# A hybrid transformer block: pooling's products, pair outputs, the first gate operands and the left operands rearranged

## The chip, the cores and the metric

The kernel runs on one core of a Trainium2 chip. A time is the device time of one execution in microseconds (us). The kernel before took 1178.16 us, the median of three runs (1177.86 to 1179.1). About 0.2% is what a measurement of this kernel can tell from no change.

## The reference

One layer of a streaming encoder on 1024 tokens of width 1024, all in float32:

1. An RMSNorm, then one input projection whose columns feed three token mixers: causal pooling (four groups of 64 channels: trailing mean over 2, 4, 8 or 16 tokens minus the input, a 64 x 64 product per group, a scale), gated linear attention (4 heads of 64, chunks of 64, a gate and a norm per head) and forgetting attention (8 heads of 64, softmax of q k + F_t - F_s under a causal mask).
2. The mixers' outputs, 256 + 256 + 512 channels, go through the output projection w_o and are added to x.
3. A second RMSNorm, then a SwiGLU feed-forward of width 2816: silu(h Wg) * (h Wu) times W_down, added to x.
4. A last RMSNorm.

## The kernel before, in words

**Precision by splitting.** TensorE takes operands in a shorter float format here (fp32r). An operand is therefore split: the high part is a copy into that format (ScalarE), the low part the difference (VectorE or POOL, the subtract). A product is three matmuls: high x high, high x low, low x high (gemm, woven, L133 to L149). Each split costs ScalarE one pass and VectorE or POOL another.

**Buffers.** SBUF is cut into 33 general buffers of 128 x 1024 and some rings (L24 to L28). `G(name)` takes the first buffer of a first-in-first-out list, `free` puts it at the end, `R` goes round a ring. This happens when the program is written down, so which name follows which in a buffer is fixed there:

```
i = idle.pop(0)
t_ = big.tile([P, 1024], dtype, tag=f"g{i}", name=name)
```

A name waits for the name before it in its buffer to be finished with, transfers included.

**Order of the work.** A planner puts the instructions of each engine in order ahead of time, by a model of their durations: among those that it thinks ready, the one that stands first in the program goes first. On the chip each engine keeps that order. So matmuls of a later step fill holes of an earlier one where the planner saw them, and the program's order is a priority. All transfers but a few are issued by SyncE's queue (SP), in one order too: one that waits for its source or its buffer holds all behind it.

**PSUM** has eight banks: three "s", two "pt", one "o", two "gm". All input and output projections use the two "gm" banks.

**Stages** (names as in the profile):

- First norm and transposes (hT, in 16 buffers), the small projections gv and a (psg), decays.
- `pool_in` projects pooling's two halves (zp0, zp1). `pool_tile` (L476) builds the shifted sums on VectorE (ps2 to ps16), then d (pd), two matmuls with w_pool (py, L500), a scaled copy on ScalarE (L501), and `keep_mix` (L265), which splits the result and stores high and low parts in memory (mixs).
- Gated linear attention in two halves, A and B (class `Gla`): `keys` (zgk), `queries` (zgq), `gates` (zgg), and small work (turn_keys, state, within, outputs, turned) handed to the projections as `smalls`, which `woven` places between their matmuls.
- `fox_values(0)` (psv), with B's last outputs between; then `keep_wo` (L273) loads, splits and stores the eight blocks of w_o (wos0 to wos7, nine general buffers in turn).
- Forgetting attention, pairs 0 to 3 of heads: `fox_qk` (zq, zk: q's and k's high and low parts into six buffers q, k, kl), `fox_attend` with eight items a pair (s scores, pt transposes, o products). For pairs 0 to 2 each item's result (oy) is stored alone (L610, mixd); the split comes later in `load_mix` (L628: mr, mix). Pair 3 is split at once into last_mix.
- Output projection in two passes: `pxa` (mix 0 to 3) between the items of pair 3, `pxb` (mix 4 to 7), followed for each of eight blocks of tokens tb by the store x3d, `norm2` (sum of squares on ScalarE, the root by `rstd_D` on VectorE and POOL, n2sq on VectorE, transposes n2pt, copies hr).
- Gate and up projections by Strassen's seven products, 22 tiles fi: `right(fi)` loads two weight blocks and makes seven right operands (five sums, seven splits), `left(i)` makes the seven left operands hA from hr, `gate_up` multiplies (m, L767). Products 3 and 5 need only the first four blocks of tokens. `start(0)` stands at tb = 4, `start(1)` behind tb = 7.
- Down projection, again by seven products (d, L1007), and the last norm.

Of the kernel before, what the change touches and what calls it, by code (L numbers as in the profile page):

```python
# [9 lines left out]
F32 = mybir.dt.float32  # L10
# [21 lines left out]
def tile_hybrid_block(ctx: ExitStack, tc, x, w_fv, w_gv, w_zt, w_o, w_gu, w_down, ln, w_pool, w_a3, chans, b_f, consts, out):  # L32
# [51 lines left out]
    POOL.memset(mhalf, -0.5)  # L84
    ACT.preload_act_table_set("natural_log_exp_and_others")
# [10 lines left out]
    def rstd_D(ms, parts, name):  # L96

        v, r = S(f"{name}_v"), S(f"{name}_r")
        extra = ms[:, 1:2] if parts == 2 else 0.0
# [161 lines left out]
    mixd = dpool.tile([3, P, T], F32, name="mixd")  # L261
    mixs = dpool.tile([4, P, 2, T], F32, name="mixs")
    wod = dpool.tile([8, P, 2, D], F32, name="wod")

    def keep_mix(k, y):  # L265

        hi, lo = R(f"mh{k}", F32R), R(f"ml{k}", F32R)
        ACT.activation(hi, y, AF.Copy)
# [207 lines left out]
    def pool_tile(j, u):  # L476
# [15 lines left out]
        d = R(f"pd{j}")  # L492
# [3 lines left out]
        y = R(f"py{j}")  # L496
        for c in range(2):
# [3 lines left out]
            ACT.activation(y[:, csl], ps, AF.Copy, scale=ch[:, 4 + j:5 + j])  # L501
        keep_mix(j, y)
        free(f"u{j}")
# [34 lines left out]
    def fox_item(p, a, m, ops, fb, V):  # L538
# [68 lines left out]
        ACT.activation(ot, o[64:128, 0:256], AF.Copy)  # L607
        DVE.tensor_tensor(out=oy[rows], in0=o[0:64, 0:256], in1=ot, op=ALU.add)
        if p < 3:
            SP.dma_start(mixd[p, rows, m * 256:(m + 1) * 256], oy[rows])  # L610
        else:
# [4 lines left out]
    def fox_attend(p, ops, V):  # L616
# [5 lines left out]
        for a, m in ([(a, m) for a in range(2) for m in range(4)] if p < 3 else [(a, m) for m in (1, 0, 3, 2) for a in range(2)]):  # L622
            fox_item(p, a, m, ops, fbs[a], V)
# [4 lines left out]
    def load_mix(k0, g):  # L628

        mixes = []  # L630
        for k in range(k0, k0 + 4):
            if k == 7:
                mixes.append(last_mix[g])
                free(f"mr6_{g}")
                break
            t_ = G(f"mix{k}_{g}", F32R).rearrange("p (h t) -> p h t", h=2)
            if k < 4:
                SP.dma_start(f(t_), mixs[k, :, :, g * 512:(g + 1) * 512])
            else:
                if k % 2 == 0:  # L640
                    raw = G(f"mr{k}_{g}").rearrange("p (k t) -> p k t", k=2)
                src = raw[:, k % 2]
                SP.dma_start(src, mixd[k - 4, :, g * 512:(g + 1) * 512])
                ACT.activation(t_[:, 0], src, AF.Copy)
                POOL.tensor_tensor(out=t_[:, 1], in0=src, in1=f(t_[:, 0]), op=ALU.subtract)
                if k % 2:
                    free(f"mr{k - 1}_{g}")
# [28 lines left out]
    for k in range(8):  # L676
        keep_wo(k)
# [422 lines left out]
```

## Time and profile before

| | |
|---|---|
| median of three runs | 1178.16 us |
| the profiled execution, its own time | 1177.12 us |
| its span | 1175.4 us |
| mean granted TensorE clock | 0.99 |

A line of the timeline reads: start in us from the span's start, length, engine, line of the kernel, operation, result <- sources, shape, count, and in brackets the idle time of the engine before it with what ended it. A line of the list of waits reads: engine and line that waited <- what released it: total, number of times, longest. A line of grouped instructions reads: line, engine, operation, operands, count | busy us, mean ns | idle us before. "PEclk" or the column after the engines in a table of stages is the clock that TensorE was granted, 1.00 being full.

### The profile page before, as it was taken

The numbers are of one execution on the slowest core, as the hardware profiler recorded it, in microseconds if no ns is written. First come the engines' busy times: TensorE is split into PE (matmuls) and PEld (weight loads), VectorE is DVE, ScalarE is ACT, GpSimd is POOL, SyncE is SP. The second block draws the span as 40 slices with busy tenths as digits, with TensorE's granted clock in tenths as the row PEclk, the third lists the DMA queues.
The fourth block names the chain that finished last, engine by engine and source line by source line (L and its number), as shares of the span: only waits on it lengthen the run. The fifth ranks groups of instructions, "written<-read, shape, count | busy, mean of one in ns | idle before, by whom it ended". The sixth has DMA issues, their size and how long they took to land.

```text
span 1175.4 us, 16005 instructions
## 1 busy us (share of the span) xinstructions
PE 1136.0 (97%) x5928; PEld 958.5 (82%) x5928; DVE 827.2 (70%) x1342; ACT 531.3 (45%) x961; POOL 353.7 (30%) x267
## 2 busy tenths in 40 slices
PE   6989999999999999898999999999999999999996
PEld 6866888889988888786888888888888888888885
DVE  7596464288757766478998768777786685876686
ACT  6345234366655444455454434443343344334344
POOL 2112032342343323231112221022201271750693
PEclk9998999999999999998999999999999999999998
DMA  7122267211205733220333232332324688333233
GB/s 250 36 73 108 91 221 263 72 46 43 64 27 170 276 122 126 99 108 25 111 107 134 91 125 71 118 123 92 118 70 152 216 321 292 104 98 107 80 118 143
DMA packets 57981, 147.31 MB, mean 125 GB/s; under 512 B 5368, under 2 KB 7336, under 8 KB 57904
## 3 DMA queue, kind: packets, MB, share of 16 engines
q1 hardware_dynamic: 57472, 144.73, 36.0%
q0 software_dynamic: 432, 1.57, 0.4%
q8 instruction: 46, 0.75, 0.3%
q14 instruction: 31, 0.25, 0.1%
HBM read 103.52 MB, written 42.76 MB: 124 GB/s over the span
## 4 chain that ended last, share of the span: by engine, by line
PE 75%; DVE 3%; issue 1%; POOL 1%; DMA 1%; ACT 1%; POOLq 0%; ACTq 0%; DVEq 0%; SPq 0%
PE m L767 35%; PE d L1007 15%; PE pxa L138 3%; PE o L604 3%; PE pxb L138 3%; PE psv L146 2%; PE pt L590 2%; PE s L564 1%; PE s L565 1%; PE zq3p L146 1%; PE zk1p L146 1%; PE zq2p L146 1%; PE zk3p L146 1%; PE zq1p L146 1%; PE zk0p L146 1%
## 5 line engine op out<-in xcount | busy, mean ns | idle before, releaser
L767 PE MATMUL m<-hA_1h,wr 128*128 128x512 f32 x616 | 215.1, 390 | 0.0
L767 PE MATMUL m<-hA_0h,wr 128*128 128x512 f32 x616 | 214.9, 391 | 0.0
L767 PEld LDWEIGHTS m<-hA_0h,wr 128*128 128x128 f32 x616 | 116.1, 189 | 24.5 <-ACT hr L727 0.3
L767 PEld LDWEIGHTS m<-hA_1h,wr 128*128 128x128 f32 x616 | 116.0, 188 | 24.3
L751 ACT ACTIVATE wr<-ws 128x512 fp32r<-128x512 f32 x110 | 69.2, 632 | 119.6 <-DVE ws L750 59.3
L767 PE MATMUL m<-hA_0l,wr 128*128 128x512 f32 x308 | 120.3, 391 | 0.0
L767 PE MATMUL m<-hA_1l,wr 128*128 128x512 f32 x308 | 120.1, 390 | 0.0
L1007 PE MATMUL d<-lw,ha 128*128 128x512 f32 x308 | 119.8, 389 | 0.0
L1007 PE MATMUL d<-hw,ha 128*128 128x512 f32 x308 | 119.3, 389 | 0.0
L1007 PE MATMUL d<-hw,la 128*128 128x512 f32 x308 | 118.3, 389 | 0.0
L819 POOL TENSOR_TENSOR cg<-cu,cu 128x512 f32<-128x512 f32 x11 | 19.6, 1778 | 306.8 <-DVE cu L796 306.8
L752 DVE TENSOR_TENSOR wr<-ws,wr 128x512 fp32r<-128x512 f32 x110 | 78.2, 718 | 25.7 <-ACT wr L751 25.7
L873 DVE TENSOR_TENSOR la<-ra,ha 128x1024 fp32r<-128x1024 f32 (+1 forms) x42 | 57.3, 1370 | 27.9 <-ACT ha L872 20.8
L865 POOL TENSOR_TENSOR rw<-wd,wd 128x512 f32<-128x512 f32 x33 | 58.5, 1800 | 49.7 <-PE d L1007 49.6
L872 ACT ACTIVATE ha<-ra 128x1024 fp32r<-128x1024 f32 (+1 forms) x42 | 41.3, 987 | 65.8 <-DMA ra<-cd 62.3
L767 PEld LDWEIGHTS m<-hA_0l,wr 128*128 128x128 f32 x308 | 58.1, 189 | 12.0
L767 PEld LDWEIGHTS m<-hA_1l,wr 128*128 128x128 f32 x308 | 57.9, 188 | 12.0
L1007 PEld LDWEIGHTS d<-lw,ha 128*128 128x128 f32 x308 | 57.8, 188 | 12.1
L1007 PEld LDWEIGHTS d<-hw,ha 128*128 128x128 f32 x308 | 57.8, 188 | 12.0
L1007 PEld LDWEIGHTS d<-hw,la 128*128 128x128 f32 x308 | 57.8, 188 | 11.9
L579 POOL TENSOR_TENSOR pb<-pb,rl 128x128 f32<-128x128 f32 (+3 forms) x32 | 38.5, 1206 | 91.3 <-DVE rl L576 73.2
L573 ACT ACTIVATE pb<-pb,mn 128x128 f32<-128x128 f32 (+3 forms) x64 | 49.5, 774 | 34.1 <-DVE mn L569 33.9
(395 smaller groups left out, 2694.7 us busy)
## 6 DMA issues: line engine op xcount, KB each, us to landing
ra<-cd SPq DMA_DIRECT2D x35, 512.0 KB, 3.9
wg<-in_w_gu_dram SPq DMA_DIRECT2D x22, 512.0 KB, 3.6
wu<-in_w_gu_dram SPq DMA_DIRECT2D x22, 512.0 KB, 4.1
wd<-in_w_down_dram SPq DMA_DIRECT2D x22, 512.0 KB, 6.9
cd<-cg SPq DMA_DIRECT2D x11, 512.0 KB, 4.5
cd<-cs SPq DMA_DIRECT2D x11, 512.0 KB, 3.3
cd<-cu SPq DMA_DIRECT2D x11, 512.0 KB, 3.3
fb<-Fd SPq DMA_DIRECT2D x8, 512.0 KB, 3.8
```

Source lines behind the costliest of these rows:

```text
L138: PE.matmul(ps, a, b, start=(n == 0), stop=(n == last))
L146: PE.matmul(ps, a, b, start=(i == 0 and n == 0), stop=(i == len(terms) - 1 and n == 2))
L573: ACT.activation(pb[:, 0:W], pb[:, 0:W], AF.Exp, bias=mn[:, 0:1], scale=-1.0, accum_out=l[:, i:i + 1])
L579: POOL.tensor_tensor(out=pb[:, 0:W], in0=pb[:, 0:W], in1=rl[:, 0:1].broadcast_to([P, W]), op=ALU.mult)
L604: PE.matmul(*args, start=(kb == 0 and n_ == 0), stop=(last and n_ == 1))
L751: ACT.activation(hi, src, AF.Copy)
L752: e2.tensor_tensor(out=lo, in0=src, in1=f(hi), op=ALU.subtract)
L767: PE.matmul(ps, a, b, start=(n == 0), stop=(n == 11))
L865: POOL.tensor_tensor(out=raw_[:, j * 512:j * 512 + 512], in0=wd[h0, j0 + j][:, e0, :], in1=wd[h1, j0 + j][:, e1, :], op=op)
L872: ACT.activation(hi[:, sl], src, AF.Copy)
L873: DVE.tensor_tensor(out=lo[:, sl], in0=src, in1=f(hi[:, sl]), op=ALU.subtract)
L1007: PE.matmul(banks[t], a[:, o], b[:, ns], start=(j0 + j == 0 and m == 0), stop=(j0 + j == NF // 2 - 1 and m == 2))
```

## The change

- Pooling: `pool_tile` still makes d at its place, but the products, their copy and `keep_mix` are returned as two small works per half. Half 1's are handed to `A.gates`, half 0's to `B.queries`. pd, py and the high part mh become general buffers instead of ring buffers; `keep_mix` writes the low part over its input. `misc` is freed later.
- Pairs 0 to 2: each item adds its result into one general buffer y{p}; when the pair is through and the next pair's q and k stand in the program, `keep_mix(4 + p)` splits and stores it. `load_mix` then loads high and low parts, with no split.
- Right operands of gate tiles 0 and 1 are made behind `keep_wo` and ahead of `fox_qk(0)` and stored in a new array rwd; at the old place `fetch_right` loads them. Their sums move from POOL to VectorE.
- Left operands 1, 4, 2, 7 and 6 are made in two halves of the tokens.
- `norm2`'s root takes its addition on POOL.

```
+    def rstd_D(ms, parts, name, eng=None):
         v, r = S(f"{name}_v"), S(f"{name}_r")
+        if eng is POOL:
+            POOL.tensor_tensor(out=v, in0=ms[:, 0:1], in1=epst, op=ALU.add)
+            POOL.tensor_tensor(out=r, in0=v, in1=mhalf[:, 0:1], op=ALU.pow)
+            return r
...
     def keep_mix(k, y):
-        hi, lo = R(f"mh{k}", F32R), R(f"ml{k}", F32R)
+        hi = G(f"mh{k}", F32R)
         ACT.activation(hi, y, AF.Copy)
-        DVE.tensor_tensor(out=lo, in0=y, in1=f(hi), op=ALU.subtract)
+        DVE.tensor_tensor(out=y, in0=y, in1=f(hi), op=ALU.subtract)
         SP.dma_start(mixs[k, :, 0], f(hi))
-        SP.dma_start(mixs[k, :, 1], f(lo))
+        SP.dma_start(mixs[k, :, 1], y)
+        free(f"mh{k}")
...
+        free(f"u{j}")
+        y = []
+        def part(c):
+            if not y:
+                y.append(G(f"py{j}"))
             csl = slice(c * 512, c * 512 + 512)
             ps = PS("s", f"py{j}_{c}")
             PE.matmul(ps, wpb[:, j, :], d[:, csl], start=True, stop=True)
+            ACT.activation(y[0][:, csl], ps, AF.Copy, scale=ch[:, 4 + j:5 + j])
+            if c:
+                keep_mix(j, y[0])
+                free(f"pd{j}", f"py{j}")
+        return [lambda c=c: part(c) for c in range(2)]
...
+        if p < 3:
+            oy = Y[:, m * 256:(m + 1) * 256]
         DVE.tensor_tensor(out=oy[rows], in0=o[0:64, 0:256], in1=ot, op=ALU.add)
-            SP.dma_start(mixd[p, rows, m * 256:(m + 1) * 256], oy[rows])
...
+    RORDER = (3, 5, 4, 1, 2, 7, 6)
+    rwd = dpool.tile([2, 7, P, 1024], F32, name="rwd")
+    def right(fi, keep=False):
...
+                DVE.tensor_tensor(out=src, in0=in0, in1=in1, op=op)
+            ACT.activation(hi, src, AF.Copy)
+            DVE.tensor_tensor(out=lo, in0=src, in1=f(hi), op=ALU.subtract)
+            ops[i] = (hi, lo)
+            if keep:
+                SP.dma_start(rwd[fi, n], f(w_))
+                free(f"wr{fi}_{i}")
+    def fetch_right(fi):
+        ops = {}
+        for n, i in enumerate(RORDER):
+            w_ = G(f"wr{fi}_{i}", F32R)
+            SP.dma_start(f(w_), rwd[fi, n])
+            ops[i] = (w_[:, 0:512], w_[:, 512:1024])
+        return ops
...
             t_ = G(f"mix{k}_{g}", F32R).rearrange("p (h t) -> p h t", h=2)
-            if k < 4:
-                SP.dma_start(f(t_), mixs[k, :, :, g * 512:(g + 1) * 512])
-            else:
...
-                SP.dma_start(src, mixd[k - 4, :, g * 512:(g + 1) * 512])
-                ACT.activation(t_[:, 0], src, AF.Copy)
-                POOL.tensor_tensor(out=t_[:, 1], in0=src, in1=f(t_[:, 0]), op=ALU.subtract)
...
+            SP.dma_start(f(t_), mixs[k, :, :, g * 512:(g + 1) * 512])
...
-    pool_tile(1, us[1])
-    pool_tile(0, us[0])
-    free("misc")
+    pools = pool_tile(1, us[1]), pool_tile(0, us[0])
-    A.gates((A.state(), A.within(0)))
+    A.gates((A.state(), pools[0] + A.within(0)))
-    B.queries((A.turned(1), B.turn_keys()))
+    B.queries((A.turned(1) + pools[1], B.turn_keys()))
+    free("misc")
...
     for k in range(8):
         keep_wo(k)
+    for fi in range(2):
+        right(fi, keep=True)
     ops = fox_qk(0)
...
+        Y = G(f"y{p}") if p < 3 else None
+        fox_attend(p, ops, V, Y)
...
         if p < 3:
             free(*done)
+            keep_mix(4 + p, Y)
+            free(f"y{p}")
...
-        r = rstd_D(ss, 1, f"n2{tb}")
+        r = rstd_D(ss, 1, f"n2{tb}", POOL)
...
+            for c in (slice(0, 256), slice(256, 512)) if max(in0, in1 or 0) > 1 else (slice(0, 512),):
+                src = raw[in0][kp][:, :, c]
+                if in1 is not None:
+                    DVE.tensor_tensor(out=t_[:, :, c], in0=src, in1=raw[in1][kp][:, :, c], op=op)
+                    src = t_[:, :, c]
+                ACT.activation(hi[:, :, c], src, AF.Copy)
+                DVE.tensor_tensor(out=lo[:, :, c], in0=src, in1=f(hi[:, :, c]), op=ALU.subtract)
...
-        w_ = right(fi)
+        w_ = fetch_right(fi) if fi < 2 else right(fi)
```

More of the change, by code (lines that the diff above doesn't have):

```diff
@@ L84, in tile_hybrid_block @@
     POOL.memset(mhalf, -0.5)
+    epst = cst.tile([P, 1], F32, name="epst")
+    POOL.memset(epst, EPS)
     ACT.preload_act_table_set("natural_log_exp_and_others")
@@ L500, in pool_tile @@
             PE.matmul(ps, wpb[:, j, :], d[:, csl], start=True, stop=True)
-            ACT.activation(y[:, csl], ps, AF.Copy, scale=ch[:, 4 + j:5 + j])
-        keep_mix(j, y)
-        free(f"u{j}")
+            ACT.activation(y[0][:, csl], ps, AF.Copy, scale=ch[:, 4 + j:5 + j])
[3 more added lines that the diff above has]
+        return [lambda c=c: part(c) for c in range(2)]
     def fox_values(q, smalls=((),) * NT):
```

67 lines of the change are left out of this document (22 added, 45 removed).

## The prediction

> **What bounds the kernel now.** I read the page's first part, then the list of who waited for whom on TensorE, then the busy time in 20 us stages, and last the timeline around each hole.
>
> ```profile
> span 1175.4 us, 16005 instructions
> PE 1136.0 (97%) x5928; PEld 958.5 (82%) x5928; DVE 827.2 (70%) x1342; ACT 531.3 (45%) x961; POOL 353.7 (30%) x267
> ...
> PE n2pt L725 <- DVE n2sq L720: 4.6, 1, 4.6
> PE py L500 <- DVE pd L495: 4.4, 1, 4.4
> PE pxb L138 <- ACT mix L644: 2.8, 1, 2.8
> PE zgq0p L146 <- ACT gk L344: 2.4, 1, 2.4
> PE pxb L138 <- DVE xa L658: 1.5, 1, 1.5
> ```
>
> TensorE is busy for all but 39 us, so an edit pays only where it fills a hole of TensorE, and every new hole is paid in full. The five long waits that the edit could touch lie in three places: pooling (py and the zgq0p behind it), the start of the output projection's second half (pxb), and the end of the second norm (n2pt). The stages price them (columns: stage, its length, then busy time and instructions of PE, PEld, DVE, ACT and POOL, granted clock, DMA share, GB/s):
>
> ```profile
> 60.00:80.00 20.00, 20.00 (x89) 16.29 (x88) 19.53 (x15) 10.18 (x14) 5.82 (x3) 1.00 0.27 88
> 80.00:100.00 20.00, 13.25 (x40) 8.64 (x39) 15.51 (x23) 7.73 (x10) 1.90 (x1) 0.83 0.27 98
> ...
> 460.00:480.00 20.00, 14.62 (x96) 11.90 (x95) 11.07 (x16) 9.80 (x21) 7.19 (x9) 1.00 0.48 172
> 480.00:500.00 20.00, 20.00 (x90) 16.31 (x90) 8.80 (x13) 7.38 (x18) 6.36 (x7) 0.92 0.38 132
> ...
> 520.00:540.00 20.00, 15.41 (x78) 12.91 (x77) 15.57 (x18) 9.53 (x21) 9.24 (x8) 0.95 0.29 106
> 540.00:560.00 20.00, 20.00 (x81) 16.17 (x81) 18.38 (x19) 12.28 (x19) 0.00 (x0) 0.88 0.09 27
> 560.00:580.00 20.00, 20.00 (x90) 16.57 (x89) 18.64 (x26) 9.56 (x13) 1.68 (x1) 1.00 0.17 52
> ```
>
> An undisturbed stage starts 89 or 90 wide matmuls, so one costs 20/90 = 0.222 us. **Pooling's hole**: 40 instead of 89 starts, 20 x 49/89 = 11.0 us; about 1.0 of it is the pooling products' own work (the four passes take 1.88 us in a warm row below, against 4 x 0.222), so 10.0 us are lost, the low clock of 0.83 included. **The projection's hole**: 20 - 14.62 = 5.4 us idle, and 8% of the next 20 us at the clock of 0.92, 1.6 us: 7.0 us. **The norm's hole**: 20 - 15.41 = 4.6 us idle, 5% of that stage for its clock, 1.0, and 9 matmuls missing in the next, 2.0 us: 7.6 us. Together 24.6 us, the most that the edit can win at these places.
>
> **The change, part by part.**
>
> Pooling's products placed later:
>
> ```profile
> 87.44 3.62 PE L500 MATMUL py<-pd,misc 128*128 128x512 f32 x4 [4.40 <-DVE pd L495]
> 88.62 1.22 DVE L113 TENSOR_TENSOR zgg0l<-zgg0r,zgg0h 128x1024 fp32r<-128x1024 f32 x1
> 96.59 0.17 DVE L495 TENSOR_TENSOR pd<-ps,u 128x16 f32<-128x16 f32 x1
> 96.84 1.90 POOL L333 TENSOR_TENSOR d<-bc 128x1024 f32<-128x1024 f32 x1 [16.97 <-DMA mixs<-ml]
> 100.86 1.88 PE L500 MATMUL py<-pd,misc 128*128 128x512 f32 x4
> 108.99 1.90 POOL L333 TENSOR_TENSOR d<-bc 128x1024 f32<-128x1024 f32 x1 [10.25 <-DMA mixs<-ml]
> ```
>
> The first py waits for VectorE's chain of shifted sums, and behind it on TensorE stand the gated attention's queries; on ScalarE the copies of py stand ahead of the copy that empties gk's bank. The edit hands the products as small work into A.gates and B.queries, at least one projection later, so both waits go. No instruction is saved; the chain of sums stays where it is. What is late next is VectorE: the two chains end at 96.59 with the zgg0 split (1.22) between, while the queries now can start where the hole began, at 87.44 - 4.40 = 83.0, and end 48 x 0.222 = 10.7 us on, at 93.7. If the second chain goes first, the key product and that split come after it, and TensorE waits up to 3.5 us: 6.5 us won. If they slip between the sums, as the split at 88.62 did, all 10.0 are won. I take 9.0, nearer to that row. The halves d2 of the keys, POOL's L333, no longer stand behind stores of pooling's outputs in their ring of buffers, which helps.
>
> Pairs' outputs split per pair: the first three head pairs now collect their output in one buffer, are split once (ScalarE and VectorE, 1024 columns) and stored in two 512 KB transfers; before, 24 stores of 64 KB, and then at the reload a split by ScalarE and POOL.
>
> ```profile
> L644 ACT ACTIVATE mix<-mr x6: 630/633/635, 373.0 to 479.0; 128x512 fp32r<-128x512 f32 x6
> L645 POOL TENSOR_TENSOR mix<-mr,mix x6: 1277/1298/1306, 373.8 to 479.8; 128x512 fp32r<-128x512 f32 x6
> ...
> 455.68 0.80 SPq L643 DMA_DIRECT2D mr<-mixd  x2
> 461.33 0.37 SPq L283 DMA_DIRECT2D wo7h<-wod  x1
> ...
> SPq L643 <- PE o L604: 14.5, 1, 14.5
> ```
>
> The load of pair 2's half (mr) waited 14.5 us for TensorE's last attention product, since its buffer was the last pair's value buffer (names handed from a first-in-first-out list; I followed that list through the code). In the changed order the first half's three mix buffers are those of k3 and kl3, read by scores and not by the last products, and 0.63 + 1.30 us of splitting goes. The weights wo7 are still issued at 461.33, so products 6 and 7 cannot start before about 465; the attention's own latency remains. Of 7.0 I take 5.5, between 2.8 (the one wait named L644) and 7.0. VectorE gets three splits of 1.22 us more, off TensorE's path in pairs 0 to 2: nothing, or 3.7 us if each is waited for.
>
> The end of the norm: right operands gone from it, lefts in halves, POOL's add in the root:
>
> ```profile
> 529.63 2.31 DVE L720 SCALAR_TENSOR_TENSOR n2sq<-xa,n_r,ln2b 128x1024 f32<-128x1024 f32 x1 [0.44 <-POOL n_r L101]
> 530.32 0.39 PE L138 MATMUL pxb<-wo7h,mix 128*128 128x512 f32 x1
> 534.75 0.68 DVE L658 TENSOR_TENSOR xa<-pxb,xa 128x512 f32<-128x512 f32 x1
> 538.89 1.94 PE L725 MATMUL n2pt<-ident,n2sq 128*128 128x128 f32 x8 [4.59 <-DVE n2sq L720]
> ```
>
> The last projection ended at 530.7, but VectorE, filled with splits of right operands that wait for POOL, added it only at 534.75; from there to the transposes 4.14 us. Without those splits the add can come at 530.8 and the transposes at 530.8 + 4.14 + about 0.5 for POOL's extra add = 535.5. TensorE has four products of 12 matmuls that need only the first half of the tokens (48 x 0.222 = 10.7 us) as cover. I take 6.0 of 7.6, from 2.0 (VectorE's left operands late, a rival below) to 7.6. The 14 reloads of 512 KB go into a stage with a DMA share of 0.29 to 0.38.
>
> Making the right operands early is where the price lies. For two tiles: 4 loads, 10 sums and 14 low parts on VectorE (24 x 0.718 = 17.2 us), 14 copies on ScalarE, 14 stores, all between the stored w_o splits and the first q/k projection. That time is free on VectorE. The **buffers** are not. At this point nine of the list's buffers are in rotation: w_o's splits leave them, the right operands take them, and q0, k0 and kl0 are then given six that right operand 1 has just used. That names wait in the order of the program, even when a buffer is free, is shown by the two L333 rows above: POOL sat idle 16.97 and 10.25 us on tiles whose inputs were long there. So the copy of q0 out of its bank waits until tile 1's operands are made and stored:
>
> ```profile
> 200.54 0.32 SPq L276 DMA_DIRECT2D wod<-wos5h  x1
> 210.47 0.59 ACT L527 ACTIVATE q<-zq0p 64x512 fp32r<-64x512 f32 x1 [6.29 <-PE zq0p L146]
> 212.44 0.69 DVE L528 SCALAR_TENSOR_TENSOR q<-zq0p,q 64x512 fp32r<-64x512 f32 x1 [0.66 <-ACT q L527]
> 215.20 0.62 PE L146 MATMUL zk0p<-hT,zk0h 128*128 128x512 f32 x2
> ...
> L751 ACT ACTIVATE wr<-ws 128x512 fp32r<-128x512 f32 x110 | 69.2, 632 | 119.6 <-DVE ws L750 59.3
> L752 DVE TENSOR_TENSOR wr<-ws,wr 128x512 fp32r<-128x512 f32 x110 | 78.2, 718 | 25.7 <-ACT wr L751 25.7
> ...
> mixs<-ml SPq DMA_DIRECT2D x4, 512.0 KB, 3.1
> wu<-in_w_gu_dram SPq DMA_DIRECT2D x22, 512.0 KB, 4.1
> ...
> DMA to landing us min/median/max: 2.6/4.2/8.8
> ```
>
> The chain: wos5h's store is issued at 200.54 and lands 3.1 later; wu0 takes its buffer, 4.1; operand 3 takes 0.72 + 0.63 + 0.72 = 2.07 and operand 5 0.72 more, to 210.5; its store 3.1; wu1 takes that buffer, 4.1; operands 3 and 5 of tile 1, 2.8, to 220.5; store 3.1, to 223.6. q0's first half could go at 222.9 and its copies take 212.44 + 0.69 - 210.47 = 2.66: the bank is empty at 225.6. Both banks of this kind hold q0, so TensorE, which went on with zk0p at 215.20, now waits 10.4 us. Behind the waiting copy on ScalarE stand the splits of zq1 and k0's copies, on SyncE the stores and behind them zq1's weights; no other matmul is ready. With stores at 4.2 (median of the w_o stores) the wait is 13.7, at 2.6 it is 8.9; I take 11.3. A cold restart comes on top, 2.0 us as after the norm's hole: **13.3 us** lost, with 0 (if I misread the list) and 27.3 (the slower rival) as bounds. The Trainium skill (TensorE: Matmul & The Clock Gate, Part 1) says that about 3.4 us without work halve the clock and about 3.4 us of work restore it. By it, as an estimate, the restart would cost 1.7 and the sum be 1170.7; the trace does not quite agree, since the projection's longest wait is 2.8 us and the clock of the next stage still reads 0.92.
>
> **Sum.** The profiled execution took 1177.12 us, 1.04 below the median shown, 1178.16. 9.0 + 5.5 + 6.0 - 13.3 = 7.2 us won: 1169.9, on the median's scale **1171.0**. Its own range: all bad ends at once are 6.5 + 2.8 + 2.0 - (13.7 + 2.0) = -4.4, all good ones 10.0 + 7.0 + 7.6 - (8.9 + 2.0) = 13.7, or 1182.6 and 1164.5; since they will hardly meet, 1166 to 1178.
>
> **Rivals.**
>
> The buffers cost nothing: the early operands hide fully, since VectorE and the DMA queues have room there. Then 20.5 us are won: 1157.7. For it: VectorE has 5.20 of 20 us to do and the DMA engines 0.46 of their time in the stage below. Against it: the chain of five transfers is latency, not share.
>
> ```profile
> 200.00:220.00 20.00, 18.84 (x93) 15.57 (x93) 5.20 (x10) 6.74 (x12) 7.13 (x3) 1.00 0.46 154
> ```
>
> Slower: the same place, but the second chain decides. The last gated output's buffer mh3 now sits ahead of wos1, wos4 and wos7:
>
> ```profile
> 197.82 1.06 ACT L268 ACTIVATE mh<-gy 128x1024 fp32r<-128x1024 f32 x1 [0.89 <-DVE gy L461]
> ```
>
> From 198.9: store 3.1, then three splits of 1.06 + 1.22 with two loads of 4.1 between, to 217.0; store 3.1, operand 6 of tile 0 in 2.07, store 3.1, operand 2 of tile 1 in 1.35, store 3.1: 229.7 for kl0, against zk0p's end at 225.6 + 5.3 = 230.9, and another 5.3 us of zk0p's second half as cover. So it decides from 236. Each of the four stores and two loads would have to take 3.4 us more (a w_o store took up to 8.8), 250 in all: a further wait of 14 us, and 1185.0. It makes the kernel slower from 9.5 us on, 1180.5.
>
> The first gate tiles become VectorE's: the left operands 1, 2, 7 and 6 need buffers of w_o that come free only with the last projection, and VectorE is already at 18.38 and 18.64 of 20 us there with TensorE never waiting. Fed 6 us sooner, TensorE waits for VectorE in the next 80 us, and the norm's gain is returned: 1177.0. For it: 3 us of slack in those two stages. Against it: VectorE, too, is free for the lefts sooner, with no splits of right operands after 530.8.
>
> **Chances and range.** Forecast 0.48, hidden buffers 0.17, the slower chain 0.19, VectorE's bound 0.16. A measurement of this kernel can tell about 0.2% from no change, 1175.8 to 1180.5. Faster: 0.42 of the forecast, all of the second, 0.05 of the last, 0.64. Slower: 0.01, 0.18 and 0.02, 0.21. The rest, 0.15, within. For 8 in 10 the range reaches from the full gain, 1157, to the slower chain's 1185.
>
> **What would show it.** The wait on py gone, and zgq0p directly behind zgk0p; no wait named L644, and pxb running between the last attention products; n2pt without a wait above 1 us; and a new wait of TensorE of about 11 us on zk0p, released by the copy of q0 (L527 and L528 of before), itself behind a store into the new array of right operands. If that wait is under 3 us, the time is near 1158 and my reading of the buffer list is wrong; if it is over 20 us, or zq1p waits as well, the kernel is slower.

## The result, and the profile after

The changed kernel takes **1210.2 us** (median of four runs, 1208.74 to 1211.09) against 1178.63 us before: a ratio of 1.0264, 95% interval 1.0246 to 1.0281. The prediction said 1171.0 with a range of 1157 to 1185. The likeliest case, a gain, did not come, and the loss is larger than the slower rival's. Of all executions below one, at 5825.72 us in the run with small stores, was slow and is left out of its median and ratio.

The page of the changed kernel, its span and first part:

```profile
span 1208.0 us, 16032 instructions
PE 1139.0 (94%) x5928; PEld 961.5 (80%) x5928; DVE 822.3 (68%) x1365; ACT 531.5 (44%) x968; POOL 333.9 (28%) x260
```

Of the other engines none does more by over 0.2 us; the span grew by 32.6 us, and TensorE's busy time and that of its weight loads (PEld) by 3.0 each. So the change made holes, not work. The list of waits of the changed kernel (engine and line that waited, what released it, total, times, longest):

```profile
PE zk0p L152 <- DVE q L541: 25.7, 1, 25.7
...
PE zgq0p L152 <- ACT gk L350: 6.8, 1, 6.8
PE n2pt L768 <- DVE n2sq L763: 3.7, 1, 3.7
PE zq0p L152 <- DVE v L531: 3.5, 1, 3.5
PE zq3p L152 <- DVE kl L546: 2.5, 1, 2.5
```

The first row is the wait that the prediction named, at its place and with its releaser, at 25.7 us in place of 11.3. The old waits on py and on the mix L644 are gone. But zgq0p, which took py's place, waits as long as both did together (4.4 and 2.4 before), n2pt has 3.7 of its 4.6 left, and two waits have grown: zq0p on a copy of the values (1.2 before) and zq3p on kl (0.2 before).

For the comparisons below I worked out from the trace how much TensorE time each stretch lost: for every matmul the time from its start to the next one's, less the median of that for its width in the same execution (227 ns for 512 columns; only what is more than 20 ns over it), summed between the first matmuls of the products named. A low clock is in it. In us:

| | keys to gates (pooling) | gates to first q | first q and k | pairs | projection, second half | end of norm | all |
|---|---|---|---|---|---|---|---|
| before | 12.4 | 18.5 | 1.3 | 10.7 | 10.0 | 7.7 | 68.4 |
| changed | 9.0 | 29.6 | 30.5 | 15.4 | 3.2 | 5.5 | 101.1 |
| difference | -3.4 | +11.1 | +29.2 | +4.7 | -6.8 | -2.2 | +32.7 |

The last column has what comes ahead and behind as well, 7.8 and 7.9 at the start. The 32.7 us account for the span.

### The profile page after: what moved, and what is told of

It is laid out like the page before. It is cut to its first block, busy times and chain, and to the rows that moved or that the text cites. A ratio compares the mean times of both kernels' runs of the same rounds, so it can differ in the third digit from the quotient of the medians.

```text
span 1208.0 us, 16032 instructions
## 1 busy us (share of the span) xinstructions
PE 1139.0 (94%) x5928; PEld 961.5 (80%) x5928; DVE 822.3 (68%) x1365; ACT 531.5 (44%) x968; POOL 333.9 (28%) x260
## 4 chain that ended last, share of the span: by engine, by line
PE 79%; DVE 7%; DMA 6%; issue 4%; ACT 2%; POOL 1%; SPq 0%; POOLq 0%; ACTq 0%; DVEq 0%
PE m L787 34%; PE d L1030 15%; PE pxa L144 4%; PE o L617 3%; PE psv L152 3%; PE pt L603 2%; PE pxb L144 2%; PE s L577 1%; PE s L578 1%; PE zk0p L152 1%; PE zgq0p L152 1%; PE psg L144 1%; PE zgk1p L152 1%; PE zgg0p L152 1%; PE zq3p L152 1%
## 5 line engine op out<-in xcount | busy, mean ns | idle before, releaser
L787 PEld LDWEIGHTS m<-hA_0h,wr 128*128 128x128 f32 x616 | 116.0, 188 | 24.4 <-ACT hr L770 0.3
L659 DVE TENSOR_TENSOR wr<-ws,wr 128x512 fp32r<-128x512 f32 x110 | 74.4, 683 | 29.9 <-ACT wr L658 29.3
L606 DVE TENSOR_TENSOR pp<-pt,pp 128x512 fp32r<-128x512 f32 (+1 forms) x80 | 50.1, 631 | 25.1 <-ACT pp L605 24.8
```

Source lines behind the costliest of these rows:

```text
L606: DVE.tensor_tensor(out=pp[:, 512:512 + w], in0=pt[:, 0:w], in1=f(pp[:, 0:w]), op=ALU.subtract)
L659: DVE.tensor_tensor(out=lo, in0=src, in1=f(hi), op=ALU.subtract)
L787: PE.matmul(ps, a, b, start=(n == 0), stop=(n == 11))
```

## The experiments

In each run the kernel before ran on the same chip; its medians there were 1178.7 to 1179.2 us.

### Each part alone

**Without the early operands.** The changed kernel, with the right operands made at the old place as before.

```
-    for fi in range(2):
-        right(fi, keep=True)
...
-        w_ = fetch_right(fi) if fi < 2 else right(fi)
+        w_ = right(fi)
```

> The changed kernel with the right operands of tiles 0 and 1 made at the old place, as before (POOL's sums, no store). Theory A: the early operands cause all of the loss of 32 us, through the wait of TensorE on q0 and the slow restart behind it; then the stage from 180 to 240 us loses about as little as before (7 us of TensorE time instead of 38), and the time is 1178 less the small gains at pooling (about 2) and the output projection (about 6), plus what the boundaries between pairs lost (about 5): 1172 to 1177. Rival B: a good part of the loss comes from the pairs' split and the moved pooling, which also shift buffers; then the stage from 180 to 240 us stays bad and the time is above 1185.

Measured: 1188.93 us, ratio 1.0088 (1.0073 to 1.0104). The stall at the first q and k is gone (1.9 us lost), so 21.3 us of the loss are the early operands'. But gates to first q still loses 29.4 and the end of the norm 11.2, so that 10 us belong to the other parts: the time is rival B's (above 1185), and theory A is right only of the wait on q0.

**The early operands alone**, on the kernel before:

> The kernel before with the early right operands alone (sums on VectorE, stores, reloads). Theory A: the wait on q0 comes as in the changed kernel, 20 to 28 us, and the norm's end wins 2 to 4: 1200 to 1207. Rival B: alone it costs less than 12 us, because in the changed kernel the last gated output's buffer ahead of the w_o blocks 1, 4 and 7 made the chain long, and here that output still goes through the ring: 1180 to 1190.

Measured: 1198.85 us, 1.0173 (1.0158 to 1.0188), between the two theories. The wait on q0 is the one below: 8 of the 25.7 us need the other parts, the rest is the operands' own.

```profile
PE zk0p L146 <- DVE q L528: 17.7, 1, 17.7
```

**The pairs' split alone:**

```
+        hi, lo = (R(f"mh{k}", F32R), R(f"ml{k}", F32R)) if k < 4 else (G(f"mh{k}", F32R), y)
...
+            keep_mix(4 + p, Y)
+            free(f"y{p}")
```

> The kernel before with the pairs' split alone: each of the first three pairs collects in one general buffer, is split once and stored; the mixes 0 to 3 keep their ring buffers. Theory A: it wins 5 to 7 us of TensorE time at the output projection's second half and pays about 5 at the boundaries between the pairs (the stages around 345 and 365 us lose 7 in the changed kernel without early operands, 3 before): 1176 to 1180. Rival B: that loss belongs to buffers shifted by the other parts, and the split is a gain: 1171 to 1174.

Measured: 1179.06 us, 0.9999 (0.9986 to 1.0012): theory A, no difference. The projection loses 4.9 in place of 10.0, but the pairs 17.2 in place of 10.7, and the end of the norm 9.5 in place of 7.7. Its waits and VectorE's timeline at the boundary:

```profile
PE zq3p L146 <- DVE kl L534: 2.5, 1, 2.5
```

```profile
350.66 1.28 DVE L534 TENSOR_TENSOR kl<-zk2p,k 64x512 fp32r<-64x512 f32 x2 [0.60 <-PE o L605]
```

VectorE could write kl2 only when TensorE's last product of pair 1 (o) was through. By the list of buffers the reason is that y1 takes one buffer out of circulation, so that both buffers of kl2 are now values of pair 1, which that product reads; before, one was. That reading was not tried in a kernel of its own. This wait, with a granted clock of 0.50 for 3.4 us behind it, makes up 4.4 of the 6.5 us that the pairs lose more (from zk2p to zk3p 7.2 in place of 2.8); the other 2 lie behind zk3p, and their cause stays open.

**Pooling alone**, with `pool_tile` and `keep_mix` as changed:

> The kernel before with pooling's part alone: products placed later, and all four mixes split in general buffers as the changed kernel does. Theory A: the hole at 80 us shrinks by only 2 (TensorE waits for gk's copy, whose ring buffer was the second shifted sum's), and the general buffers of the last gated output, ahead of the w_o block 1, hold up the copies of the values on VectorE and lose 8 to 11 us from 120 to 220 us: 1183 to 1188. Rival B: the losses from 120 to 220 us are the early operands' or the pairs': 1175 to 1178.

Measured: 1187.86 us, 1.0077 (1.0062 to 1.0092): theory A. It wins 3.1 us from keys to gates and loses 11.4 from the gates to the first q (29.9 against 18.5), as in the changed kernel.

**Left operands in halves and the root's addition on POOL alone:**

> The kernel before with the left operands in halves and POOL's addition in the second norm's root alone. Theory A: these lengthen the norm's end, as the changed kernel without early operands shows (11.2 us lost there in place of 7.8): 1180 to 1183. Rival B: they are neutral or a small gain, and the longer end comes from the moved reloads: 1175 to 1179.

Measured: 1181.51 us, 1.0029 (1.0017 to 1.0042): theory A. The end of the norm loses 9.5 in place of 7.7. VectorE's timeline there, where TensorE's last projection began its last matmul at 531.71:

```profile
535.38 1.28 DVE L900 TENSOR_TENSOR hs<-hr,hr 128x512 f32<-128x512 f32 x2
536.59 0.68 DVE L903 TENSOR_TENSOR hA_1l<-hr,hA_1h 128x512 fp32r<-128x512 f32 x1
537.19 0.68 DVE L664 TENSOR_TENSOR xa<-pxb,xa 128x512 f32<-128x512 f32 x1
```

A half can be made as soon as its tokens are there, and so the halves (hs, hA) got places ahead of the last addition (xa), for which the norm and the transposes wait. It starts 5.5 us after that matmul; before, it was 4.4 (530.32 to 534.75). More pieces that are ready early are more work ahead of the one that counts. The root, now all on POOL, costs more than that:

```profile
538.54 1.65 POOL L756 TENSOR_TENSOR ws<-wg,wu 128x512 f32<-128x512 f32 x1 [3.63 <-DVE wr L758]
540.15 0.63 POOL L102 TENSOR_TENSOR n_v<-n2ss,epst 128x1 f32<-128x1 f32 x1
```

The square was through at 539.06, but the root stood behind a sum of right operands on POOL, and n2sq came at 541.87: 2.8 us, for 0.85 before. The run has both edits in it and does not separate their times. In its profiled execution another 1.2 us are lost between keys and gates (13.6 for 12.4), where TensorE, VectorE and ScalarE have the same order as before; a difference of about 1 us in one stretch is thus no evidence.

The four parts alone cost 9.2, 0.4, 19.7 and 2.8 us: 32.1 together, against 31.6 measured for all. That they agree so well is in part chance, since the parts do act on each other: the wait on q0 is 17.7 us alone and 25.7 together.

### Pooling: two buffers

**Gated outputs back in the ring.** Pooling alone again, but the mixes 2 and 3 are split into ring buffers, as before.

```
+        ring = k in (2, 3)
+        hi, lo = (R(f"mh{k}", F32R), R(f"ml{k}", F32R)) if ring else (G(f"mh{k}", F32R), y)
```

> Pooling's part alone, as run before, but the two gated outputs are split into ring buffers again, as in the kernel before; only pooling's own two products use general buffers. Theory A: the loss from 160 to 220 us (20 us of TensorE time there in place of 10) comes from the last gated output's buffer ahead of the w_o block 1, whose late split holds the copies of the values on VectorE; with ring buffers it goes back to about 10, and the time is 1176 to 1179. Rival B: the loss comes from the moved products and their splits themselves, which stand among the gates' and queries' work: 1184 or more.

Measured: 1178.87 us, 0.9999 (0.9988 to 1.0011): theory A; the stretch from the gates to the first q is back at 20.5. The changed kernel's timeline shows what the general buffer did (ScalarE, then VectorE):

```profile
207.07 1.06 ACT L118 ACTIVATE wos1h<-wos1r 128x1024 fp32r<-128x1024 f32 x1 [0.15 <-DMA mixs<-mh]
208.16 2.33 DVE L119 TENSOR_TENSOR wos1l<-wos1r,wos1h 128x1024 fp32r<-128x1024 f32 x1 [1.87 <-ACT wos1h L118]
210.41 0.47 DVE L531 TENSOR_TENSOR v<-psv,v 128x128 fp32r<-128x128 f32 x2
```

The split of w_o block 1, which is needed only some 200 us later, waits for the store of the gated output (mh) in its buffer, and behind its second half on VectorE stand the value copies (v), for which TensorE waits 3.5 us.

**A buffer of its own for gk.** The same, and the key's copy gk in a general buffer.

```
-            j, k_ = self.j, R(f"gk{self.j}")
+            j, k_ = self.j, G(f"gk{self.j}")
```

> The kernel of the run beside it, and the key's copy gk in a general buffer in place of a ring buffer. Theory A: the hole at 80 us stays at 9 in the changed kernel because gk's ring buffer is that of the second shifted sum, so that its copy waits for VectorE's chain; with a buffer of its own the queries start when the keys end, and the hole falls to 3 to 5: 5 to 7 us faster than the run beside it. Rival B: VectorE, at 19.8 of 20 us there, or ScalarE's order is the bound, and the hole stays at 8 to 10: within 2 us of the run beside it.

Measured: 1174.89 us, 0.9965 (0.9951 to 0.9979). The same kernel run again:

> The kernel before with pooling's products moved, the gated outputs in ring buffers and gk in a general buffer: the same kernel as the run at 1174.9, beside the one-tile kernel on one chip. It should come 3 to 5 us under the kernel before again, 1174 to 1176; at 1178 or more that gain was scatter.

Measured: 1175.43 us, 0.9978 (0.9968 to 0.9987). The hole falls from 10.0 (the run before) to 4.7 and 4.4, as theory A had it, though the time gains 4.0 us on that run and not 5 to 7; and it is **a version faster than both kernels**, 3.4 to 4.0 us under the kernel before. In the changed kernel the hole looked so (VectorE, POOL, ScalarE, TensorE):

```profile
81.72 2.91 DVE L486 TENSOR_TENSOR ps<-u 128x1023 f32<-128x1023 f32 x1
...
85.82 1.21 DVE L486 TENSOR_TENSOR ps<-ps 128x1022 f32<-128x1022 f32 x1
...
87.11 1.89 POOL L339 TENSOR_TENSOR d<-bc 128x1024 f32<-128x1024 f32 x1 [3.56 <-DVE ps L500]
87.14 2.94 DVE L486 TENSOR_TENSOR ps<-ps 128x1020 f32<-128x1020 f32 x1
...
90.17 0.60 ACT L350 ACTIVATE gk<-zgk0p 128x512 f32<-128x512 f32 x1 [5.53 <-DVE ps L486]
...
90.82 1.22 PE L152 MATMUL zgq0p<-hT,zgq0h 128*128 128x512 f32 x2 [6.84 <-ACT gk L350]
```

The copy of gk is released by the end of a shifted sum, not by the keys' last matmul: its ring buffer is the second shifted sum's, which the third (87.14) reads. In the faster kernel the longest waits left, behind that of the first norm, are the end of the second norm and gk's use:

```profile
PE n2pt L735 <- DVE n2sq L730: 5.1, 1, 5.1
PE pk L373 <- DVE d L348: 3.8, 1, 3.8
```

### The early operands: bytes, order, place

**Small stores.** The changed kernel; an early operand's store writes 4 of 128 partitions, and the operands are made once more at the old place.

```
-                SP.dma_start(rwd[fi, n], f(w_))
+                SP.dma_start(rwd[fi, n, 0:4], f(w_)[0:4])
...
-        w_ = fetch_right(fi) if fi < 2 else right(fi)
+        w_ = right(fi)
```

> The changed kernel, but each early operand's store writes 4 of 128 partitions (16 KB in place of 512 KB), and the operands are made once more at the old place, as before; loads, sums, splits, buffers and their order stay. Theory A (the transfers' bytes): the stores of 7.3 MB fill the DMA engines at about 400 GB/s from 205 to 250 us, so that each transfer of the chain takes 8 us in place of 3 to 4; without them the wait on zk0p falls from 25.7 to under 10 us. Rival B (order: the second tile's operands stand behind the split of the w_o block 7 on ScalarE, and that block waits for a chain of w_o blocks 1 and 4): the chain is there without the bytes too, and the wait stays at 14 us or more.

Measured: 1213.27 us (median of three), 1.0298 (1.0278 to 1.0317); the wait on zk0p is 19.5 us: theory B. The kernel as a whole is no faster than the changed one because the operands are made again at the norm, whose end loses 12 us here. Its stages of 5 us within that wait:

```profile
225.00:230.00 5.00, 0.00 (x0) 0.00 (x0) 1.23 (x1) 1.13 (x2) 2.24 (x1) 0.81 0.94 335
230.00:235.00 5.00, 0.00 (x0) 0.00 (x0) 2.37 (x4) 2.27 (x4) 0.00 (x0) 0.50 0.73 297
235.00:240.00 5.00, 0.00 (x0) 0.00 (x0) 4.39 (x8) 2.98 (x7) 0.00 (x0) 0.50 0.06 11
```

With 7.1 MB less to store, 6.2 us of the wait went. In the last row the DMA engines are idle and VectorE is busy for 4.39 of 5 us, with TensorE still waiting: there it is the operands' work that stands ahead of q0's copies. Up to 235 us the other transfers alone keep the share at 0.73 to 0.94, so this run does not show how long the chain would be with the DMA engines free.

**q and k first.** The changed kernel, with the operands written behind the first pair's q and k and its output buffer.

```
-    for fi in range(2):
-        right(fi, keep=True)
     ops = fox_qk(0)
     free("gv0", "gv1", "attb0", "attb1")
+    Y0 = G("y0")
+    for fi in range(2):
+        right(fi, keep=True)
```

> The changed kernel with the early right operands written behind the first pair's q and k, and behind the pair's output buffer, so that these get their buffers and their places in the order first; the work is the same, the bytes too. Theory A (what counts is who stands first for buffers and in the engines' order, not the bytes): no wait on q0, the stretch from 200 to 240 us loses 6 us as without early operands, 1179 to 1190. Rival B: the operands stand ahead of the first pair's attention in the program, and their 17 us on VectorE and their stores come back as waits between 240 and 320 us: 1195 to 1210.

Measured: 1202.67 us, 1.0204 (1.0188 to 1.0219): theory B. The first q and k lose 1.7 us in place of 30.5, but the pairs 34.9 in place of 15.4. The stage in which most of it falls:

```profile
260.00:280.00 20.00, 10.08 (x43) 7.68 (x42) 19.74 (x43) 12.70 (x30) 4.93 (x4) 0.66 0.53 212
```

VectorE is busy for 19.74 of 20 us, and TensorE's longest new wait is for it:

```profile
PE s L577 <- DVE mn L582: 6.2, 6, 2.0
```

The stall thus goes when q0 stands first, in buffers and in the engines' order together; the work then needs VectorE's time where there is no room.

**Behind the pairs.** The changed kernel with the operands behind the last pair in the program.

> The changed kernel with the early right operands made behind the last pair in the program and ahead of the w_o reloads, where hT's sixteen buffers have just come free, in place of ahead of the first pair. Theory A (place and buffers were the trouble, not the work): no wait on q0, the 17 us of VectorE's work and the stores hide beside the last pair, and the norm's end keeps its gain: 1166 to 1173. Rival B: the stores and the first items of the last pair collide (the DMA engines have 0.5 to 1.0 share where the w_o blocks come back), and TensorE waits for w_o or for VectorE by 5 to 15 us: 1178 to 1188.

Measured: 1238.04 us, 1.0500 (1.0483 to 1.0518), the worst of all. A wait and SyncE's queue:

```profile
PE pxa L144 <- DMA mix<-mixs: 28.4, 2, 24.4
```

```profile
446.46 13.83 SPq L686 DMA_DIRECT2D mix<-mixs  x2
461.49 2.85 SPq L662 DMA_DIRECT2D rwd<-wr  x2
...
472.78 0.53 SPq L686 DMA_DIRECT2D mix<-mixs  x1
```

The second load of the first row was issued only at 459.77, when TensorE's last attention product (o) had freed its buffer. Behind it the operands' stores began, at 461.49, and the load that ended the wait of 24.4 us went out at 472.78, behind six of these stores, and landed at 484.1, at a DMA share of 1.02 from 470 to 480. Theory B was right in kind (the stores collide with what the last pair needs), though it was the mixes that came late, and its 5 to 15 us were far too few.

**Ahead of the second half's gates**, on the kernel before, and then on the changed kernel:

```
+    for fi in range(2):
+        right(fi, keep=True)
     B.gates((B.state(), B.within(0)))
```

> The kernel before with the early right operands alone, written ahead of the second half's gates (about 110 us) in place of behind the w_o blocks (about 205 us). There VectorE works 6.7 to 13 of each 20 us and the DMA engines carry 79 to 215 GB/s. Theory A (the work needs free time on VectorE and ahead of a buffer's next user): no wait on q0, and the norm's end wins about 2 as in the run with the operands behind w_o: 1174 to 1178. Rival B: the values and the w_o blocks now follow the operands in their buffers and in SyncE's queue, and lose 5 us or more between 150 and 210 us: 1182 or more.

> The changed kernel with nothing but the early right operands' place altered: ahead of the second half's gates in place of behind the w_o blocks. Theory A: the wait on q0 was made by the place; the time is that without early operands, 1188.9, less 3 to 6 at the norm's end: 1183 to 1187. Rival B: in the changed kernel only eight general buffers are left there, pooling's second product and the last gated output among their users, and the operands make a new wait of 10 us or more: 1195 to 1210.

Measured: 1178.43 us, 0.9998 (0.9984 to 1.0011), and 1185.70 us, 1.0060 (1.0040 to 1.0080). Theory A in the second: the same work at another place costs 24.5 us less than in the changed kernel. It is 3.2 under the kernel with no early operands, but the two ran on different chips and their intervals overlap. In the first, 0.4 us outside theory A's range and far from B's, the end of the norm falls to 3.0 us lost, from 7.7, and 1.6 to 1.7 are paid each from the gates to the first q and there; the time is unchanged. Its wait and VectorE's timeline at the last norm, whose last projection began its last matmul at 534.47:

```profile
PE n2pt L764 <- ACT hr L766: 0.9, 1, 0.9
```

```profile
534.90 0.69 DVE L695 TENSOR_TENSOR xa<-pxb,xa 128x512 f32<-128x512 f32 x1 [1.86 <-PE pxb L138]
```

The addition follows the projection at once. So the early operands do at the norm what the prediction said of them. In the changed kernel the addition followed at once as well (568.21, the last matmul at 567.78); it loses 5.5 us there for 3.0 because the transposes come 4.7 us after it, for 4.2 here, and because the granted clock is 0.50 from 573 to 576, where here it stays at 1.00 from 536 to 544.

### Parts put together

> The kernel before with two parts: pooling's products moved, with the gated outputs in ring buffers and gk in a general buffer (the run at 1174.9), and the early right operands written ahead of the second half's gates (the run in which the norm's end lost 3.0 us of TensorE time in place of 7.8). Theory A: the gains add, 4 from pooling and 4.8 from the norm's end less 3 lost at the first q projection: 1171 to 1174. Rival B: both take general buffers in the same stretch, the values or the w_o blocks wait for them, and the sum is no better than pooling alone: 1175 to 1182.

> The changed kernel with the operands ahead of the second half's gates, the gated outputs in ring buffers, gk in a general buffer, left operands whole and the root's addition on VectorE: the two parts of the run beside it and the pairs' split. Theory A: the split wins 5 to 7 at the projection and loses 4 to 5 at the boundary of pairs 1 and 2, where kl2 takes both value buffers of pair 1: within 2 us of the run beside it. Rival B: with the norm's end clear the projection's gain reaches the end, and the kernel is 3 to 6 us faster than the run beside it.

> Pooling's products moved with the ring buffers and gk's own buffer (as in the run beside it), and only tile 0's seven right operands made early, ahead of the second half's gates; tile 1's stay at the old place. Theory A: the splits that held up the last norm are tile 0's, so half of the work wins most of the norm's end (8 us lost to 3 to 5), and half of the buffers, stores and VectorE's work costs less between the gates and the first q (33 us lost with both tiles, 22 with none): 3 to 5 us faster than the run beside it. Rival B: one late buffer is enough to hold the values, the gates' stretch loses 28 or more, and the kernel is no faster than the run beside it.

Measured: 1180.87 us, 1.0011 (1.0000 to 1.0022), for pooling's fix with both tiles early; 1184.53 us, 1.0043 (1.0027 to 1.0059), with the pairs' split as well; 1176.35 us, 0.9978 (0.9969 to 0.9986), for pooling's fix with one tile early, against 1175.43 for pooling's fix alone on the same chip. Rival B in the first and the last; in the middle one both were wrong, as it was 3.7 us slower than its neighbour. The gains do not add:

| | keys to gates | gates to first q | end of norm | all |
|---|---|---|---|---|
| pooling's fix | 4.4 | 21.4 | 8.1 | 66.0 |
| and one tile early | 4.0 | 28.0 | 4.6 | 67.4 |
| and both tiles early | 4.5 | 32.6 | 3.0 | 72.0 |

Each tile wins 1.6 to 3.5 us at the norm and pays 4.6 to 6.6 ahead of the first q. With both tiles the wait there is this one:

```profile
PE psv L146 <- DVE v L529: 7.1, 2, 4.8
```

## Why the prediction was wrong, step by step

**Bound and method.** That TensorE sets the time and that each new hole is paid in full was right: the holes add up to the difference. By the table of lost time, what lies between forecast and result (39.2 us) is 15.9 of the new stall (29.2 for 13.3), 11.1 from the gates to the first q and 4.7 at the pairs, both put at nothing, 5.6 at pooling and 3.8 at the norm, less 1.3 that the projection won over its forecast, 39.8 in all.

**Pooling's hole, +9.0.** Wrong: 3.4 us won there, and 11 paid behind it. The step that failed is that "the queries now can start where the hole began". py's wait went, but the copy of gk had a second condition, its ring buffer; I followed the general list of buffers by name and looked at the rings only for d2. The kernel before (VectorE, VectorE, ScalarE):

```profile
82.39 1.21 DVE L480 TENSOR_TENSOR ps<-ps 128x1020 f32<-128x1020 f32 x1
...
91.20 0.69 DVE L491 COPY ps<-ps 64x1024 f32<-64x1024 f32 x1
...
92.78 1.07 ACT L344 ACTIVATE gk<-zgk0p 128x512 f32<-128x512 f32 x2
```

By the order in which the ring is handed out, gk's buffer was that of half 0's second sum (last read at 91.20), and the copy followed at 92.78, behind the split of py on ScalarE. With pd, py and their splits out of the ring, gk got the buffer of half 1's second sum, which the third reads. And that sum moved from 82.39 to 87.14, behind sums of half 0, so "the chain of sums stays where it is" was wrong too: at its old place it would have been through at 83.6, near the 83.0 of the prediction. The 11 us are a cost that I priced only inside a rival: the gated outputs in general buffers, ahead of w_o. Undoing that and giving gk its own buffer brought the kernel to 1175. At the hole itself 7.7 to 8.0 us are then won (12.4 to 4.7 and 4.4), near the 9.0; the kernel gains 3.4 to 4.0, since part of it is paid again, 2.9 to 3.9 from the gates to the first q (21.4 and 22.4 for 18.5). The first L333 row was misread as well: by the same order d2's buffer was a shifted sum's, whose last use ended at 96.76 (96.59 + 0.17), and not one of a store.

**Projection's hole, +5.5.** The size was right: 6.8 won in the changed kernel, 5.1 in the part alone. The step that failed is the price of the split, "nothing, or 3.7 us if each is waited for": I costed VectorE's time and not the buffer that y holds through a whole pair. The pairs lose 4.7 us in the changed kernel and 6.5 in the part alone, and that returns the gain. That the buffer is the reason is read from the list and one row, and was not tried.

**The norm's tail, +6.0.** 2.2 won. The latency was as worked out: the addition came at 568.21 and the transposes at 572.93, 4.7 us, for 4.14 + 0.5. But the 0.5 was met by luck. It was meant for POOL's addition, and from the end of the square to n2sq are 0.9 us (570.57 to 571.50), as before (536.61 to 537.46). The square itself began 1.2 us after the addition, for 0.7 before, behind two copies of hr that had stood behind it:

```profile
568.88 0.66 ACT L770 ACTIVATE hr<-n2pt 128x256 f32<-128x256 f32 x2 [0.16 <-PE n2pt L768]
569.42 1.06 ACT L761 ACTIVATE n2sq<-xa 128x1024 f32<-128x1024 f32 x1
```

The step that failed is the cover, "TensorE has four products of 12 matmuls": the trace starts 24 of those matmuls, two products, ahead of the last transposes, before and after. In the changed kernel 23 of the 24 ran ahead of the last projection's last matmul, since their operands came sooner, and one was left to cover the 4.7 us; before, 12 were. The halves and the root on POOL, which lengthen the tail in their run alone, do not show here: POOL had no sums of right operands left in its way.

**The new stall, -13.3.** The place, the releaser and the reason (q0's buffer, behind the operands) were right, the size was not: 29.2 us, 25.7 of them the wait itself, for 11.3. ScalarE's timeline in the changed kernel, then SyncE's:

```profile
215.06 0.63 ACT L658 ACTIVATE wr<-wu 128x512 fp32r<-128x512 f32 x1 [3.87 <-DMA wu<-in_w_gu_dram]
...
231.28 1.06 ACT L118 ACTIVATE wos7h<-wos7r 128x1024 fp32r<-128x1024 f32 x1 [6.83 <-DMA wos7r<-in_w_o_dram]
233.73 0.63 ACT L658 ACTIVATE wr<-wu 128x512 fp32r<-128x512 f32 x1 [1.40 <-DMA wu<-in_w_gu_dram]
...
237.46 0.63 ACT L658 ACTIVATE wr<-ws 128x512 fp32r<-128x512 f32 x1 [2.58 <-DMA wod<-wos7h]
238.71 0.63 ACT L658 ACTIVATE wr<-ws 128x512 fp32r<-128x512 f32 x1 [0.62 <-DMA wod<-wos7l]
239.57 0.63 ACT L658 ACTIVATE wr<-ws 128x512 fp32r<-128x512 f32 x1 [0.23 <-DVE ws L657]
...
245.71 0.63 ACT L658 ACTIVATE wr<-ws 128x512 fp32r<-128x512 f32 x1 [0.84 <-DVE ws L657]
246.25 1.05 ACT L540 ACTIVATE q<-zq0p 64x512 fp32r<-64x512 f32 x2
```

```profile
208.28 0.89 SPq L646 DMA_DIRECT2D wu<-in_w_gu_dram  x1
...
222.79 1.10 SPq L117 DMA_DIRECT2D wos7r<-in_w_o_dram  x1
223.98 1.07 SPq L646 DMA_DIRECT2D wu<-in_w_gu_dram  x1
```

Against the chain of the prediction: wu0's load was issued at 208.28 for 203.6, 4.6 us late, because the gated output, whose store stands ahead in SyncE's queue, came 4.5 us later (mh at 202.34 for 197.82); its data was used 6.8 us later, for 4.1. wu1 was issued at 223.98, behind w_o block 7 in SyncE's queue, for 213.6; its data came 9.75 us later, for 4.1. From there to q0's copy are 12.5 us, for 5.2. Operand 3 of tile 1, whose buffer q0 takes, got its high part only at 239.57, since operands 7 and 6 of tile 0 stood ahead of it on ScalarE (237.46 and 238.71) and waited for the stores of w_o block 7; its own store went at 240.95 and landed at 244.94, 4.0 us for 3.1; and the copy of q0 then stood 1.3 us behind the last operand on ScalarE. So three terms were mis-sized: the start of the chain, the transfers, and the work ahead of operand 3. "The chain of five transfers is latency, not share" is the sentence that was wrong: I took the DMA engines' share of 0.46 from before and did not add the change's own 9.4 MB to it. The run with small stores puts 6.2 us of the wait down to the stores' bytes, the run with the early operands alone 8.0 to the other parts; whether the two add up was not tried. The row of landing times "2.6/4.2/8.8" was misread too: it has the reloads of w_o in it, and the stores of the high parts alone took 2.6 to 3.6.

**The slower rival.** Its wait of 14 us more, 27.3 in all, is near the measured 29.2, and its chain (mh3, then w_o blocks 1, 4 and 7) is the one that ScalarE's rows at 207.07 and 231.28 show; its condition, 3.4 us more for a transfer, was met (block 7's load was issued at 222.79 and used at 231.28, 8.5 us for 4.1). It differs at the end: it reached q0, through the operands that stood behind block 7 on ScalarE, and not kl0. Its time of 1185.0 kept gains that did not come. VectorE as the bound of the first gate tiles did not show up: no matmul there waits in the changed kernel's list.

## What to carry to other kernels

Where names share buffers in the program's order, moving work moves the waits of names that have nothing to do with it: list for each buffer touched who has it next, in rings as well, and how soon that one is needed. As far as these runs go, work that is early and not urgent must stand behind the next urgent thing in buffers, in each engine's order and in the DMA queue, all three; being free on one engine is not enough. And test the parts of a change one by one, down to the buffers: pooling's part lost 9.2 us as it was written, and won 3.4 to 4.0 with two of its buffers chosen anew.

## What the runs showed of the hardware

**The clock came back late.** The changed kernel in stages of 5 us (the column after the engines is the granted clock, then DMA share and GB/s):

```profile
225.00:230.00 5.00, 0.00 (x0) 0.00 (x0) 0.00 (x0) 0.00 (x0) 1.87 (x1) 0.80 1.03 421
230.00:235.00 5.00, 0.00 (x0) 0.00 (x0) 1.83 (x2) 2.21 (x3) 0.00 (x0) 0.50 0.99 367
...
245.00:250.00 5.00, 0.72 (x2) 0.65 (x3) 4.55 (x8) 2.77 (x5) 0.00 (x0) 0.50 1.01 405
250.00:255.00 5.00, 5.00 (x14) 3.84 (x13) 0.00 (x0) 0.00 (x0) 0.00 (x0) 0.50 0.07 26
255.00:260.00 5.00, 5.00 (x23) 4.13 (x22) 0.82 (x2) 1.18 (x2) 1.28 (x3) 0.97 0.02 3
```

TensorE started again about 0.7 us ahead of 250 (its busy time in that row) and ran at 0.50 until past 255, some 6 us, of which half is lost: 3 us for the restart, where the prediction took 2.0. The Trainium skill (TensorE: Matmul & The Clock Gate, Part 1) gives about 3.4 us of sustained work, in a window that runs free; this restart took longer than one such window.

**The transfers were full at about 400 GB/s.** In the same rows the share is 0.99 to 1.03 at 367 to 421 GB/s. The Trainium skill (Perfetto Trace Analysis, Roofline) puts a single core's DMA engines at about 435 GB/s together; the trace agrees so far as no row here is above it.

**A VectorE sum beside a POOL one.** The rows of pooling's hole above: a shifted sum of 1022 columns takes 1.21 us alone, and the next, of 1020 columns, 2.94 when POOL's L339 (1.89 us) has started 0.03 us ahead of it, 1.73 more. The Trainium skill (SBUF — State Buffer, SBUF: two separate sides) says that the port pair which both use is held for a whole instruction and the other engine waits; the trace agrees.
